# Attention's probabilities times values: from split float32r on the whole array to plain float32 on two column halves

## The chip, the core and the metric

The kernel runs on one core of a Trainium2 chip. A core has five engines with a queue of instructions each: TensorE (PE in the profile, with its weight loads as PEld), VectorE (DVE), ScalarE (ACT), GpSimd (POOL) and SyncE (SP), which here issues the DMAs. Arrays lie in SBUF, 128 partitions with a free axis; TensorE writes to PSUM only, here six tiles that the kernel calls banks. The metric is device time in microseconds (us) of one execution, the median of several runs. One execution was also taken with the hardware profiler; all durations below are from it.

## What is computed

Two layers of a hybrid mixer, over 1024 latent tokens and 256 context tokens of width 1024. One input projection feeds a convolution branch, windowed attention and a gated linear attention (GLA); each branch has its own gate, and an output projection ends the layer. What matters here is the attention:

```python
def one_block(args):                       # 128 queries, 8 heads, 2 kv heads
    qn, kn, vn, mn = args
    s_loc = jnp.einsum('bqhgd,bkhd->bhgqk', qn, kn).astype(F32)
    s_loc = jnp.where(mn, s_loc, NEG_INF)
    s_ctx = jnp.einsum('bqhgd,bchd->bhgqc', qn, kc).astype(F32)
    p = jax.nn.softmax(jnp.concatenate([s_sink, s_ctx, s_loc], axis=-1), axis=-1)
    return (jnp.einsum('bhgqc,bchd->bqhgd', p_ctx, vc)
            + jnp.einsum('bhgqk,bkhd->bqhgd', p_loc, vn))
b_l = _windowed_attention(...) * jax.nn.silu(pl['b_gate'])
```

A block of 128 queries looks at the 256 context tokens and at its own, the previous and the next 128 tokens. In layer 0 the two context blocks attend as well, to the context alone. Everything is float32.

## The kernel before

The kernel is written as some dozens of generators ("lanes") which a planner runs (`Hybrid.loop`, lines 201 to 228). `Model` (lines 49 to 154) holds an estimated clock of each engine and, for every eight columns of a buffer, when it will be written and read; a lane yields what it waits for, and the planner resumes the lane with the smallest priority number among those that are ready at the model's PE clock, or else the one that will be ready first. The order in which instructions are issued is therefore set at build time by these estimates. A matmul with a `tile_position` is priced at its full cost times its share of the columns plus 29 ns (line 141); the model has no price for going from whole-array matmuls to tiled ones and back.

Precise products use float32r, a float32 type that TensorE takes in one pass. An operand is split into a high part (rounded to float32r) and a low part (what is left), and three products, high-high, high-low and low-high, are summed (`three`, line 673); `split` (line 362) does it with a copy and a subtraction.

The attention phase of a layer starts at `attn_start` (line 1187). Its units are (query block, kv head) with four heads each: 20 in layer 0, 16 in layer 1. A unit (`u_run`, line 1304) makes scores for four heads (`u_score`), takes exponentials and sums (`u_head`), scales them, and then goes over its 128-token key tiles, 5 for an inner block, 4 for a border block, 2 for a context block, which is 84 pairs of unit and key tile in layer 0 and 76 in layer 1, 160 in all. For each pair four TensorE transposes (one per head) fill a PSUM bank with 128 keys by 512 (head, query) columns. `u_ev` (line 1379) brings the bank to SBUF as a PT buffer of 1024 columns: ACT copies it, halved, into float32r, then DVE subtracts that copy from the bank to get the low part. `u_pv` (line 1388) multiplies: the stationary operand is `vst`, 128 keys by 128 columns that hold the high and the low part of one kv head's values, and the moving operand is the high and then the low half of PT, two matmuls of 512 columns that accumulate over the unit's key tiles in a bank `O`. Rows 0 to 63 of `O` then hold the high values' products and rows 64 to 127 the low values'; ACT copies the lower half out, DVE adds the halves (twice, one for each parity of the head), and DVE or POOL multiplies the result into the gate in `mix`.

The values get to `vst` by `v_prep` (line 1253): a DMA from the DRAM tensor `kd` to a small buffer, then a split. There are 3 PT buffers, cut from `H1`, the 8192-column float32r tile that held the projection's input for tokens 0 to 511; they are free once its last reader, the gate group `(7, 1)` in `phase_a`, has been issued (flag `h1out`). `H1` also holds the odd query tile, and `hi` and `ml`, the split operands of the output projection (`out_tiles`, line 1469).

Lanes of priority below the units' (2 and up) are `u_pv` (1.8), `u_ev` (1.7), `u_head` (1.9) and the preparation of keys and queries (1); the gate groups (9) and the output projection (8) fill in. Banks for transposes are limited to 3 at a time during the gate groups and after (`CAPB`, `CAPC`), accumulators to 2 and then 3.

Of the kernel before, what the change touches and what calls it, by code (L numbers as in the profile page):

```python
# [9 lines left out]
F32 = mybir.dt.float32  # L10
F32R = mybir.dt.float32r
# [153 lines left out]
class Hybrid:  # L165
# [361 lines left out]
    def views(self):  # L527

        self.HC = self.tile("HC", 4096, F32R)
        self.H2 = [self.tile(f"H2_{k}", 4096, F32R) for k in range(2)]  # L530
        for k in range(3):
            self.slots["PT"].append((0.0, self.H1[:, 2560 + 1024 * k:3584 + 1024 * k]))
        self.hc = self.HC.rearrange("p (s k t) -> p s k t", s=2, k=8)
        self.h2 = [x.rearrange("p (s k t) -> p s k t", s=2, k=4) for x in self.H2]

    def H(self, c, hl, k, a, n):
        if c == 0:
            return self.hc[:, hl, k, a:a + n]
        if c == 1:
            return self.h1[:, hl, k, a:a + n]  # L540
        return self.h2[k // 4][:, hl, k % 4, a:a + n]

    def rstd(self, ss, scale, n):
# [14 lines left out]
    def part_h(self, l, i, k0, n, x):  # L558

        nc = self.nc  # L560
        c, a = self.hslot(i)
        st = 1 if i < 2 else 0
        mods = tuple(f"mod{l}.{m + k // 2}" for m in (0, 4) for k in range(k0, k0 + n, 2))
        yield mods if n == 2 else mods[0]
        yield self.bank_need("tr")
        tp = self.bank_get("tr")
        for b in range(n):
            nc.tensor.transpose(tp[:, b * 128:(b + 1) * 128], x[:, b * 128:(b + 1) * 128], self.idf)
        yield None, self.need("SM"), mods, f"hfree{l}{c}"
        h = self.sm(128 * n)  # L570
        v = []
        for b in range(n):
            k = k0 + b
            v.append((h[:, b * 128:(b + 1) * 128], tp[:, b * 128:(b + 1) * 128],
                      self.modc[:, l, 8 + k, st:st + 1], self.modc[:, l, k, st:st + 1]))

        def on_dve():
            for o, p, s, f in v:
                nc.vector.tensor_scalar(o, p, s, f, op0=ALU.mult, op1=ALU.add)

        def on_act():
            for o, p, s, f in v:
                nc.scalar.activation(o, p, ACTF.Identity, scale=s, bias=f)
        self.pick(("dve", 320 * n, on_dve), ("act", 345 * n, on_act))
        self.free(tp)
        yield
        t = self.h2[k0 // 4][:, :, k0 % 4:k0 % 4 + n] if c == 2 else (self.hc if c == 0 else self.h1)[:, :, k0:k0 + n]
        self.split(t[:, 0, :, a:a + 128], t[:, 1, :, a:a + 128], h.rearrange("p (b t) -> p b t", b=n))
        self.free(h)
        for k in range(k0, k0 + n, 2):  # L590
            self.flag(f"h{l}.{i}.{k // 2}")
# [595 lines left out]
    def attn_start(self, l):  # L1187

        nc = self.nc
        kv = self.H1  # L1190
        self.kst = self.HC[:, 0:3072].rearrange("p (v s t) -> p v s t", v=2, s=2)
        self.vst = kv[:, 0:1536].rearrange("p (t v c) -> p t v c", t=6, v=2)
        self.Q = [x.rearrange("p (h t) -> p h t", h=8) for x in (self.HC[:, 3072:4096], kv[:, 1536:2560])]
        self.ml = kv[:, 7680:8192].rearrange("p (a b t) -> p a b t", a=2, b=2)
        yield self.need("SM", 1, 0, True), tuple(f"{x}{l}.{i}" for x in ("kv", "q0", "q1") for i in range(2, NT))
        self.rope_free()
        self.amask = self.sm(640)
        self.rsv = True
        nc.sync.dma_start(self.amask, self.I["amask"])
        self.go(self.gate_rows(l), 3)  # L1200
        ctx = [0, 1] if l == 0 else []
        blocks = list(range(2, NT)) + ctx if CTXL else ctx + list(range(2, NT))
        prev = None
        for n, i in enumerate(blocks):
            for kv in range(2):
                u = self.unit(l, n, i, kv, prev)
                self.units.append(u)
                u.lane = self.go(self.u_run(u), 2 + 0.01 * len(self.units))
                prev = u
        self.outs = self.go(self.out_proj(l, blocks), 8)  # L1210
        done = set()
        for n, i in enumerate(blocks):
            for t in self.keys(i):
                if t not in done:
                    done.add(t)
                    yield f"kv{l}.{t}", lambda: 0.0 if self.pre < 4 else None
                    self.pre += 1
                    self.go(self.kv_prep(l, t, blocks.index(t - 3) if t >= 6 else None), 1)
            yield f"q0{l}.{i}", f"q1{l}.{i}", lambda: 0.0 if self.pre < 4 else None
            self.pre += 1  # L1220
            self.go(self.q_prep(l, n, i), 1)
# [29 lines left out]
        self.flag(f"k{l}.{i}")  # L1251

    def v_prep(self, l, i, used):
        nc = self.nc
        j = self.kslot(i)
        yield self.need("SM", 1, PK), f"h1out{l}", *used
        x = self.sm_spare(128)
        nc.sync.dma_start(x, self.kd[i, :, 128:256])
        yield self.at(x)
        self.split(self.vst[:, j, :, 0:64], self.vst[:, j, :, 64:128], x.rearrange("p (v d) -> p v d", v=2))  # L1260
        self.free(x)
        self.flag(f"kv{l}.{i}.v")

    def q_prep(self, l, n, i):
# [114 lines left out]
    def u_ev(self, u, q, tp, PT):  # L1379
        nc = self.nc  # L1380
        yield self.at(tp)
        nc.scalar.activation(PT[:, 0:512], tp, ACTF.Copy, scale=0.5)
        yield
        nc.vector.scalar_tensor_tensor(PT[:, 512:1024], tp, 0.5, PT[:, 0:512].bitcast(F32), op0=ALU.mult, op1=ALU.subtract)
        self.free(tp)
        u.PT[q] = (PT, nc.end)

    def u_pv(self, u):
        nc = self.nc
        nk = len(u.keys)  # L1390
        O = None
        for q in range(nk):
            yield lambda: u.PT[q][1] if q in u.PT else None, (0.0 if q else self.bank_need("ac"))
            if q == 0:
                O = self.bank_get("ac")
            PT = u.PT[q][0]
            for s in range(2):
                nc.tensor.matmul(O, self.vst[:, self.kslot(u.keys[q]), u.kv], PT[:, s * 512:(s + 1) * 512], start=(q == 0 and s == 0),
                                 stop=(q == nk - 1 and s == 1))
            self.free(PT)  # L1400
        yield None, self.need("SM"), tuple(f"bg{u.l}.{2 + 2 * u.kv}.{j}.{self.hslot(u.i)[0]}" for j in (0, 1))
        tt = self.sm(512)
        nc.scalar.activation(tt[0:64], O[64:128], ACTF.Copy)
        yield
        O4 = O.rearrange("p (a b t) -> p a b t", a=2, b=2)
        t4 = tt.rearrange("p (a b t) -> p a b t", a=2, b=2)
        for b in (1, 0):
            nc.vector.tensor_tensor(t4[64 * b:64 * b + 64, :, 0], O4[0:64, :, b], t4[0:64, :, b], op=ALU.add)
        self.free(O)
        yield  # L1410
        c = col(u.i * 128)
        g = self.mix(slice(2 + 2 * u.kv, 4 + 2 * u.kv), slice(c, c + 128))
        self.pick(("dve", 345, lambda: nc.vector.tensor_tensor(g, g, t4[:, :, 0], op=ALU.mult)),
                  ("pool", 690, lambda: nc.gpsimd.tensor_tensor(g, g, t4[:, :, 0], op=ALU.mult)))
        self.free(tt)
        self.flag(f"u{u.key}")


# [50 lines left out]
    def out_tiles(self, l, blocks, par, lanes):  # L1469
        yield  # L1470
        for n, i in list(enumerate(blocks))[par::2]:
            early = par == 0 and n < len(blocks) - 4
            lanes[par].prio = 8 + 0.01 * n
            if l == 0 and n >= len(blocks) - 2:
                a = 256 + 256 * par
                hi = self.HC[:, 0:3072].rearrange("p (a c) -> p a c", a=4)[:, :, a:a + 256].rearrange("p a (b t) -> p a b t", b=2)
                free = f"sc{l}.{len(blocks) - 3}"
            else:
                a = 5632 + 1024 * par
                hi = self.H1[:, a:a + 1024].rearrange("p (a b t) -> p a b t", a=4, b=2)  # L1480
                free = f"h1out{l}"
            yield (self.need("SM", 2 - early, 1), f"u{l}.{n}.0", f"u{l}.{n}.1", free, f"gb{l}",
                   f"ln{l}{self.hslot(i)[0]}", self.rest(hi), (self.rest(self.ml) if early else 0.0))
# [88 lines left out]
    def phase_a(self, l):  # L1572
# [9 lines left out]
        for g in GROUPS[:-1]:  # L1582
# [34 lines left out]
            else:  # L1617
# [4 lines left out]
                for n, (p, c) in enumerate(B_GATE):  # L1622
# [2 lines left out]
                    yield from self.t_group(l, p, self.ev_gate(l, 2 * p - 10), cx, order=(c,), last=all(x[0] != p for x in B_GATE[n + 1:]))  # L1625
                    if n == MODG:
                        self.flag("mods")
                    if p == 7:
                        self.flag({0: f"hcfree{l}", 1: f"h1out{l}", 2: f"h2out{l}"}[c])

    def phase_bc(self, l):
# [8 lines left out]
                self.go(self.x_next(i), 1 + 0.01 * ((i - 2) % NT))  # L1640
        yield tuple(u.lane for u in self.units), f"ml{l}.0", f"ml{l}.1"
        self.slots["SF"] = []
        self.flag(f"hfree{l + 1}1")
        self.free(self.amask)
        yield self.outs
# [9 lines left out]
    def run(self):  # L1655
        nc, I = self.nc, self.I
        self.w, self.gk, self.zs = {}, {}, {}
        with self.tc.manual_schedule():
            self.consts()
            self.stat = self.sb.tile([128, 4, 2, 4], F32, name="stat")  # L1660
            self.mix_new(F32)
            self.H1 = self.tile("H1", 8192, F32R)
            self.h1 = self.H1.rearrange("p (s k t) -> p s k t", s=2, k=8)
            self.flag("hfree01")

            def x_load(i):
# [73 lines left out]
PK = 1  # L1740
# [95 lines left out]
```

## Time and profile before

| | |
|---|---|
| median of 3 runs | 1324.24 us (1323.89 to 1325.28) |
| the profiled execution | 1324.96 us, span of its core 1323.2 us |
| PE busy | 1245.2 us, 94% of the span |
| PEld / DVE / ACT / POOL busy | 1085.2 / 931.4 / 600.4 / 490.8 us |
| granted TensorE clock, mean | 0.985 of full speed |
| attention of layer 0, of layer 1 | about 440 to 700 us and 1080 to 1290 us of the span |

A matmul's row begins when its columns start into the array and has an end that is modelled, so rows of successive matmuls overlap: a matmul of 256 columns is listed with some 280 ns although the next one starts 120 ns later. What a matmul costs PE is therefore read from start to start. In the profile one float32 matmul counts as two instructions (two passes), a float32r matmul and a transpose as one. Line 43 is the helper through which every instruction is issued, so rows are told apart by their tiles: `H` stands for H1 and H2 (numbers are left out), `SM` are small work buffers, `idr` is the identity of a transpose, `WS` weights, `mix` the gates and branch outputs.

### The profile page before, as it was taken

What the parts mean: (1) busy time and instruction counts of PE and PEld (TensorE: products, weight loads), DVE (VectorE), ACT (ScalarE), POOL (GpSimd) and SP (SyncE); (2) the same over time, 40 slices, a digit from 0 to 9 for tenths busy, and PEclk for the clock granted to TensorE, in tenths of its full rate; (3) what the DMA queues carried; (4) which work ended last, traced back from release to release, by engine and by line L of the source; (5) the groups of instructions that cost most, each with busy time, mean ns of one, the idle gap of its engine ahead of it and who ended that gap; (6) DMA issues with size and microseconds to landing.
All of it is one profiled execution on the core that took longest, in us unless ns stands there. A gap on an engine that the chain in (4) does not pass through costs nothing. (4 is left out here: it accounts for less than half of the span.)

```text
span 1323.2 us, 24344 instructions
## 1 busy us (share of the span) xinstructions
PE 1245.2 (94%) x9198; PEld 1085.2 (82%) x9198; DVE 931.4 (70%) x1756; ACT 600.4 (45%) x1355; POOL 490.8 (37%) x657
## 2 busy tenths in 40 slices
PE   5999998999999999899999899989999999899997
PEld 3668987888887777779988779878888888799887
DVE  5836896886364578767686677897864667987874
ACT  3721441254323456457664451431343256776641
POOL 1410054754133335434441231064651344455420
PEclk9999998999999999999999999989999999999999
DMA  9443113222014243431114521114321131211012
GB/s 327 153 140 118 48 41 96 57 76 79 28 44 142 92 131 99 138 109 51 49 57 144 182 90 59 45 42 116 85 64 56 44 97 41 87 62 53 33 65 80
DMA packets 113238, 116.48 MB, mean 88 GB/s; under 512 B 38464, under 2 KB 81760, under 8 KB 113120
## 3 DMA queue, kind: packets, MB, share of 16 engines
q1 hardware_dynamic: 113120, 114.92, 28.3%
q8 instruction: 72, 1.18, 0.4%
q14 instruction: 46, 0.38, 0.1%
HBM read 95.47 MB, written 19.42 MB: 87 GB/s over the span
## 5 line engine op out<-in xcount | busy, mean ns | idle before, releaser
L43 PE MATMUL ps<-H,WS 128*128 128x512 f32 x1344 | 338.0, 399 | 3.3 <-ACT U L43 1.7
L43 PEld LDWEIGHTS ps<-H,WS 128*128 128x128 f32 x1344 | 245.2, 189 | 62.2 <-issue 8.8
L43 PE MATMUL ps<-WS,H 128*128 128x256 f32 x1704 | 256.6, 292 | 6.6 <-DVE H L43 3.5
L43 PEld LDWEIGHTS ps<-WS,H 128*128 128x128 f32 x1704 | 229.4, 195 | 20.0 <-issue 10.3
L43 ACT ACTIVATE SM<-ps 128x512 f32<-128x512 f32 (+3 forms) x180 | 93.0, 517 | 333.8 <-PE ps L43 291.9
L43 DVE SCALAR_TENSOR_TENSOR mix<-U,small,mix 128x1295 f32<-128x1295 f32 (+1 forms) x120 | 177.8, 1522 | 0.0
L43 PE MATMUL ps<-idr,SM 128*128 128x128 f32 (+1 forms) x1076 | 150.1, 272 | 26.8 <-POOL SM L43 14.2
L43 PEld LDWEIGHTS ps<-idr,SM 128*128 128x128 f32 (+1 forms) x1076 | 124.3, 143 | 51.3 <-POOL SM L43 17.2
L43 ACT ACTIVATE SM<-SM,stat 128x641 f32<-128x641 f32 (+2 forms) x144 | 110.6, 769 | 50.5 <-DVE stat L43 38.0
L43 DVE SCALAR_TENSOR_TENSOR H<-ps,H 128x512 fp32r<-128x512 f32 x160 | 106.0, 682 | 38.1 <-ACT H L43 37.8
L43 ACT ACTIVATE H<-ps 128x512 fp32r<-128x512 f32 x174 | 98.6, 597 | 73.6 <-PE ps L43 63.7
L43 DVE CUSTOM_DVE_ANT_0 SM<-ps,SM,small 128x640 f32<-128x640 f32 (+2 forms) x128 | 102.5, 810 | 29.1 <-PE ps L43 28.4
L43 POOL TENSOR_TENSOR tir<-tir,mhalf 128x1 f32<-128x1 f32 (+2 forms) x55 | 46.5, 851 | 178.8 <-DVE tir L43 154.1
L43 POOL TENSOR_TENSOR SM<-SM,SM 128x128 fp32r<-128x128 f32 (+3 forms) x58 | 58.6, 1018 | 130.8 <-ACT SM L43 108.9
L43 PE MATMUL ps<-H 128*128 128x512 f32 x320 | 97.5, 406 | 1.4 <-DVE H L43 1.3
L43 PE MATMUL ps<-H,H 128*128 128x256 f32 x552 | 98.2, 286 | 0.2 <-DVE H L43 0.2
L43 ACT ACTIVATE SM<-SM 32x128 f32<-32x128 f32 (+4 forms) x200 | 72.0, 368 | 41.2 <-DVE SM L43 33.5
L43 PE MATMUL ps<-SM,SM 128*32 128x128 f32 (+4 forms) x764 | 79.2, 288 | 7.5 <-ACT SM L43 3.9
L43 PEld LDWEIGHTS ps<-H,H 128*128 128x128 f32 x552 | 82.0, 189 | 2.1 <-DVE H L43 0.5
L43 POOL TENSOR_SCALAR SM<-SM,tir 128x640 f32<-128x640 f32 (+2 forms) x77 | 64.7, 853 | 34.5 <-DVE tir L43 23.9
L43 POOL TENSOR_TENSOR SM<-SM,WR 128x256 f32<-128x256 f32 (+2 forms) x66 | 69.0, 1051 | 16.0 <-DVE SM L43 5.8
L43 POOL TENSOR_TENSOR WR<-SM,SM 128x256 f32<-128x256 f32 (+1 forms) x48 | 45.5, 969 | 72.1 <-ACT SM L43 72.1
(151 smaller groups left out, 2133.3 us busy)
## 6 DMA issues: line engine op xcount, KB each, us to landing
WR<-in_w_in_dram SPq DMA_DIRECT2D x80, 256.0 KB, 3.7
WR<-in_w_mod_dram SPq DMA_DIRECT2D x64, 256.0 KB, 3.1
WR<-in_w_out_dram SPq DMA_DIRECT2D x32, 256.0 KB, 3.3
SM<-vd SPq DMA_DIRECT2D x116, 64.0 KB, 2.5
x<-SM SPq DMA_DIRECT2D x20, 256.0 KB, 2.4
SM<-x SPq DMA_DIRECT2D x20, 256.0 KB, 4.0
qd<-SM SPq DMA_DIRECT2D x18, 256.0 KB, 2.4
mix<-in_x_dram SPq DMA_DIRECT2D x8, 512.0 KB, 8.3
```

What stands on the lines that cost most here:

```text
L43: r = getattr(self._e, op)(*a, **k)
```

## The change

`H1` becomes two tiles of 4096 columns, one for the high and one for the low part. When gate group `(7, 1)` has been issued, the high one is taken again as a float32 tile (`h1_keep`): 768 columns for the values and six PT buffers of 512 columns. The odd query tile, `hi` and `ml` move to the low one. Probabilities and values are no longer split. `v_prep` becomes one DMA from `kd` straight to `vst`. `u_ev` becomes one copy, halved, on ACT or on DVE, whichever the planner expects to end first. In `u_pv` each key tile has two float32 matmuls of 256 columns: heads of even parity go to array columns 0 to 63, those of odd parity to columns 64 to 127 (`tile_position`), so that `O` gets 128 rows and 256 columns, and one DVE multiplication from PSUM into the gate ends the unit. The transposes, scores, softmax and projections are not edited; since the planner's estimates change, the order in which everything is issued may change too.

```diff
-        for k in range(3):
-            self.slots["PT"].append((0.0, self.H1[:, 2560 + 1024 * k:3584 + 1024 * k]))
...
+    def h1_keep(self):
+        self.h1_new(0, F32)
+        x = self.H1[0]
+        self.vst = x[:, 0:768].rearrange("p (t v c) -> p t v c", t=6, v=2)
+        for k in range(6):
+            p = x[:, 768 + 512 * k:1280 + 512 * k]
+            self.slots["PT"].append((self.nc.touched(p), p))
...
     def v_prep(self, l, i, used):
-        nc = self.nc
-        j = self.kslot(i)
-        yield self.need("SM", 1, PK), f"h1out{l}", *used
-        x = self.sm_spare(128)
-        nc.sync.dma_start(x, self.kd[i, :, 128:256])
-        yield self.at(x)
-        self.split(self.vst[:, j, :, 0:64], self.vst[:, j, :, 64:128], x.rearrange("p (v d) -> p v d", v=2))
-        self.free(x)
+        yield f"h1out{l}", *used
+        self.nc.sync.dma_start(self.vst[:, self.kslot(i)], self.kd[i, :, 128:256].rearrange("p (v c) -> p v c", v=2))
...
     def u_ev(self, u, q, tp, PT):
-        nc.scalar.activation(PT[:, 0:512], tp, ACTF.Copy, scale=0.5)
-        yield
-        nc.vector.scalar_tensor_tensor(PT[:, 512:1024], tp, 0.5, PT[:, 0:512].bitcast(F32), op0=ALU.mult, op1=ALU.subtract)
+        self.pick(("act", 135 + 512 / 1.4, lambda: nc.scalar.activation(PT, tp, ACTF.Copy, scale=0.5)),
+                  ("dve", 75 + 512 / 0.96, lambda: nc.vector.tensor_scalar(PT, tp, 0.5, None, op0=ALU.mult)))
...
     def u_pv(self, u):
...
-            for s in range(2):
-                nc.tensor.matmul(O, self.vst[:, self.kslot(u.keys[q]), u.kv], PT[:, s * 512:(s + 1) * 512], start=(q == 0 and s == 0),
-                                 stop=(q == nk - 1 and s == 1))
+            p4 = PT.rearrange("p (a b t) -> p a b t", a=2, b=2)
+            for b in range(2):
+                nc.tensor.matmul(O[64 * b:64 * b + 64], self.vst[:, self.kslot(u.keys[q]), u.kv], p4[:, :, b], start=(q == 0),
+                                 stop=(q == nk - 1), tile_position=(0, 64 * b))
             self.free(PT)
-        yield None, self.need("SM"), tuple(f"bg{u.l}.{2 + 2 * u.kv}.{j}.{self.hslot(u.i)[0]}" for j in (0, 1))
-        tt = self.sm(512)
-        nc.scalar.activation(tt[0:64], O[64:128], ACTF.Copy)
...
-        for b in (1, 0):
-            nc.vector.tensor_tensor(t4[64 * b:64 * b + 64, :, 0], O4[0:64, :, b], t4[0:64, :, b], op=ALU.add)
...
-        self.pick(("dve", 345, lambda: nc.vector.tensor_tensor(g, g, t4[:, :, 0], op=ALU.mult)),
-                  ("pool", 690, lambda: nc.gpsimd.tensor_tensor(g, g, t4[:, :, 0], op=ALU.mult)))
+        nc.vector.tensor_tensor(g, O, g, op=ALU.mult)
...
-                a = 5632 + 1024 * par
-                hi = self.H1[:, a:a + 1024].rearrange("p (a b t) -> p a b t", a=4, b=2)
+                a = 1024 + 1024 * par
+                hi = self.H1[1][:, a:a + 1024].rearrange("p (a b t) -> p a b t", a=4, b=2)
...
+                    if (p, c) == (7, 1):
+                        self.h1_keep()
...
+        if l == 0:
+            self.slots["PT"] = []
+            self.h1_new(0, F32R)
```

## Rows read from the trace of the kernel before

**Rows 1.** The page: busy time; then 40 equal slices, in tenths.
```profile
PE 1245.2 (94%) x9198; PEld 1085.2 (82%) x9198; DVE 931.4 (70%) x1756; ACT 600.4 (45%) x1355; POOL 490.8 (37%) x657
...
PE   5999998999999999899999899989999999899997
...
PEclk9999998999999999999999999989999999999999
```

**Rows 2.** Busy time by stretch: the two attentions, the ends of the layers.
```profile
core 0: us, PE busy (x) PEld busy (x) DVE busy (x) ACT busy (x) POOL busy (x), PEclk, DMA share, GB/s
440.00:700.00 260.00, 249.60 (x1789) 215.74 (x1788) 191.11 (x409) 154.61 (x340) 109.51 (x184) 0.99 0.30 95
1080.00:1290.00 210.00, 200.37 (x1431) 181.77 (x1430) 168.49 (x345) 139.26 (x296) 95.86 (x156) 1.00 0.18 59
```

**Rows 3.** Groups of instructions: busy us, mean ns of one, idle before.
```profile
L43 PE MATMUL ps<-H 128*128 128x512 f32 x320 | 97.5, 406 | 1.4 <-DVE H L43 1.3
...
L43 DVE SCALAR_TENSOR_TENSOR H<-ps,H 128x512 fp32r<-128x512 f32 x160 | 106.0, 682 | 38.1 <-ACT H L43 37.8
...
L43 DVE TENSOR_TENSOR SM<-ps,SM 64x256 f32<-64x256 f32 x72 | 30.1, 418 | 11.3 <-ACT SM L43 9.2 <-issue 1.0
...
L43 DVE CAST HC<-ps 128x512 fp32r<-128x512 f32 x6 | 4.1, 687 | 6.0 <-PE ps L43 6.0
...
L43 ACT ACTIVATE H<-ps 128x512 fp32r<-128x512 f32 x174 | 98.6, 597 | 73.6 <-PE ps L43 63.7 <-DVE stat L43 4.4 <-DVE H L43 3.5
```

**Rows 4.** Timeline of PE: one product amid output projection, layer 1.
```profile
1258.18 0.40 PE L43 MATMUL ps<-WS,H 128*128 128x256 f32 x2
1258.41 0.28 PE L43 MATMUL ps<-WS,SM 128*128 128x256 f32 x1
1258.53 0.40 PE L43 MATMUL ps<-WS,H 128*128 128x256 f32 x2
1258.77 0.28 PE L43 MATMUL ps<-WS,SM 128*128 128x256 f32 x1
1258.88 0.63 PE L43 MATMUL ps<-H 128*128 128x512 f32 x2
1259.35 0.63 PE L43 MATMUL ps<-HC,H 128*128 128x256 f32 x4
```

**Rows 5.** Timeline of PE in GLA: column-half products amid a projection.
```profile
253.46 1.08 PE L43 MATMUL ps<-SM,SM 128*64 128x256 f32 x8
254.48 1.69 PE L43 MATMUL ps<-WS,HC 128*128 128x256 f32 x12
256.10 1.08 PE L43 MATMUL ps<-SM,SM 128*64 128x256 f32 x8
257.01 0.40 PE L43 MATMUL ps<-mix,SM 128*64 128x64 f32 x4
...
277.24 0.65 PE L43 MATMUL ps<-SM,SM 128*64 128x256 f32 x4 [0.64 <-ACT SM L43]
277.82 1.45 PE L43 MATMUL ps<-WS,H 128*128 128x256 f32 x10
...
315.76 1.52 PE L43 MATMUL ps<-SM,SM 128*64 128x256 f32 x12
```

**Rows 6.** Timeline of PE: first and last runs of attention's products.
```profile
447.97 0.63 PE L43 MATMUL ps<-H 128*128 128x512 f32 x2
...
448.73 1.16 PE L43 MATMUL ps<-H 128*128 128x512 f32 x4
449.72 1.35 PE L43 MATMUL ps<-idr,SM 128*128 128x128 f32 x12
...
1283.57 0.63 PE L43 MATMUL ps<-H 128*128 128x512 f32 x2
```

**Rows 7.** Waits of PE's weight loads, 440 to 700, then 1080 to 1290.
```profile
PEld ps L43 <- ACT ps L43: 5.9, 4, 2.4
PEld ps L43 <- DVE H L43: 3.1, 5, 1.2
PEld ps L43 <- ACT H L43: 2.0, 6, 0.4
...
PEld ps L43 <- DVE H L43: 9.8, 13, 2.1
PEld ps L43 <- DVE stat L43: 3.6, 7, 0.8
```

More of the change, by code (lines that the diff above doesn't have):

```diff
@@ L530, in views, with h1_new @@
         self.H2 = [self.tile(f"H2_{k}", 4096, F32R) for k in range(2)]
-        for k in range(3):
-            self.slots["PT"].append((0.0, self.H1[:, 2560 + 1024 * k:3584 + 1024 * k]))
         self.hc = self.HC.rearrange("p (s k t) -> p s k t", s=2, k=8)
         self.h2 = [x.rearrange("p (s k t) -> p s k t", s=2, k=4) for x in self.H2]
+    def h1_new(self, s, dt):
+        t, old = self.tile(f"H1_{s}", 4096, dt), self.H1[s]
+        if old is not None:
+            m, b = self.nc.part(t)
+            m[1, b] = self.nc.touched(old)
+        self.H1[s] = t
+        if dt == F32R:
+            self.h1[s] = t.rearrange("p (k t) -> p k t", k=8)
+    def h1_keep(self):
[5 more added lines that the diff above has]
+            self.slots["PT"].append((self.nc.touched(p), p))
     def H(self, c, hl, k, a, n):
@@ L539, in H @@
         if c == 1:
-            return self.h1[:, hl, k, a:a + n]
+            return self.h1[hl][:, k, a:a + n]
         return self.h2[k // 4][:, hl, k % 4, a:a + n]
@@ L586, in part_h @@
         yield
-        t = self.h2[k0 // 4][:, :, k0 % 4:k0 % 4 + n] if c == 2 else (self.hc if c == 0 else self.h1)[:, :, k0:k0 + n]
-        self.split(t[:, 0, :, a:a + 128], t[:, 1, :, a:a + 128], h.rearrange("p (b t) -> p b t", b=n))
+        if c == 1:
+            t = [x[:, k0:k0 + n, a:a + 128] for x in self.h1]
+        else:
+            t = [(self.h2[k0 // 4][:, s, k0 % 4:k0 % 4 + n] if c else self.hc[:, s, k0:k0 + n])[:, :, a:a + 128] for s in range(2)]
+        self.split(*t, h.rearrange("p (b t) -> p b t", b=n))
         self.free(h)
@@ L1189, in attn_start @@
         nc = self.nc
-        kv = self.H1
         self.kst = self.HC[:, 0:3072].rearrange("p (v s t) -> p v s t", v=2, s=2)
-        self.vst = kv[:, 0:1536].rearrange("p (t v c) -> p t v c", t=6, v=2)
-        self.Q = [x.rearrange("p (h t) -> p h t", h=8) for x in (self.HC[:, 3072:4096], kv[:, 1536:2560])]
-        self.ml = kv[:, 7680:8192].rearrange("p (a b t) -> p a b t", a=2, b=2)
+        self.Q = [x.rearrange("p (h t) -> p h t", h=8) for x in (self.HC[:, 3072:4096], self.H1[1][:, 0:1024])]
+        self.ml = self.H1[1][:, 3072:3584].rearrange("p (a b t) -> p a b t", a=2, b=2)
         yield self.need("SM", 1, 0, True), tuple(f"{x}{l}.{i}" for x in ("kv", "q0", "q1") for i in range(2, NT))
@@ L1390, in u_pv @@
         nk = len(u.keys)
-        O = None
+        bank = None
         for q in range(nk):
@@ L1394, in u_pv @@
             if q == 0:
-                O = self.bank_get("ac")
+                bank = self.bank_get("ac")
+                O = bank[:, 0:256].rearrange("p (a t) -> p a t", a=2)
             PT = u.PT[q][0]
-            for s in range(2):
-                nc.tensor.matmul(O, self.vst[:, self.kslot(u.keys[q]), u.kv], PT[:, s * 512:(s + 1) * 512], start=(q == 0 and s == 0),
-                                 stop=(q == nk - 1 and s == 1))
+            p4 = PT.rearrange("p (a b t) -> p a b t", a=2, b=2)
+            for b in range(2):
+                nc.tensor.matmul(O[64 * b:64 * b + 64], self.vst[:, self.kslot(u.keys[q]), u.kv], p4[:, :, b], start=(q == 0),
+                                 stop=(q == nk - 1), tile_position=(0, 64 * b))
             self.free(PT)
-        yield None, self.need("SM"), tuple(f"bg{u.l}.{2 + 2 * u.kv}.{j}.{self.hslot(u.i)[0]}" for j in (0, 1))
-        tt = self.sm(512)
-        nc.scalar.activation(tt[0:64], O[64:128], ACTF.Copy)
-        yield
-        O4 = O.rearrange("p (a b t) -> p a b t", a=2, b=2)
-        t4 = tt.rearrange("p (a b t) -> p a b t", a=2, b=2)
-        for b in (1, 0):
-            nc.vector.tensor_tensor(t4[64 * b:64 * b + 64, :, 0], O4[0:64, :, b], t4[0:64, :, b], op=ALU.add)
-        self.free(O)
-        yield
+        yield None, tuple(f"bg{u.l}.{2 + 2 * u.kv}.{j}.{self.hslot(u.i)[0]}" for j in (0, 1))
         c = col(u.i * 128)
         g = self.mix(slice(2 + 2 * u.kv, 4 + 2 * u.kv), slice(c, c + 128))
-        self.pick(("dve", 345, lambda: nc.vector.tensor_tensor(g, g, t4[:, :, 0], op=ALU.mult)),
-                  ("pool", 690, lambda: nc.gpsimd.tensor_tensor(g, g, t4[:, :, 0], op=ALU.mult)))
-        self.free(tt)
+        nc.vector.tensor_tensor(g, O, g, op=ALU.mult)
+        self.free(bank)
         self.flag(f"u{u.key}")
@@ L1661, in run @@
             self.mix_new(F32)
-            self.H1 = self.tile("H1", 8192, F32R)
-            self.h1 = self.H1.rearrange("p (s k t) -> p s k t", s=2, k=8)
+            self.H1, self.h1 = [None, None], [None, None]
+            for s in range(2):
+                self.h1_new(s, F32R)
             self.flag("hfree01")
```

## The prediction

> **What bounds the kernel now.** I began with the page's busy times [rows 1]: PE is busy for 94% of the span and its granted clock is full nearly everywhere, while DVE, the next, stands at 70%. Then the stretches [rows 2]. The change touches only the two attention phases. In the first PE is busy for 249.6 of 260 us, in the second for 200.4 of 210, with DVE at 191.1 and 168.5. So DVE is loaded but PE is the engine that runs out of time, and an edit is worth what it does to PE: its own work, or its waits. Next the waits of PE's queue in the two stretches [rows 7]: what PE waits for among the attention's own products (a PT half that DVE or ACT has still to write, named H) is 3.1 + 2.0 + 9.8 = 14.9 us; the rest of the list is bank copies and softmax statistics, 5.9 and 3.6 us in the largest rows. The reader is to see that the large DVE group (160 subtractions, 106.0 us, [rows 3]) is hidden behind PE except for those 14.9 us.
>
> **What a product costs PE before.** From start to start [rows 4]: projection matmuls of 256 columns follow each other at 0.117 us (1258.18 to 1258.53, three of them). The product of one key tile, two float32r matmuls of 512 columns, takes 1258.88 to 1259.35, 0.47 us, and nothing is lost before or after it. The 160 of them are about 75 us; the 97.5 us of [rows 3] contain waits and overlaps.
>
> **What it costs after.** GLA already has the same thing: float32, 256 columns, 64 array columns, the two halves in turn [rows 5]. Four records are one pair of such matmuls, which is what one key tile will need. A group of 4 lasts 0.65 us, of 8 1.08, of 12 1.52: each further pair adds (1.52 - 0.65)/2 = 0.435 us, that is, two steps of some 0.217 us for four passes. The two halves do run side by side. Streaming gains 0.47 - 0.435 = 0.035 us for a key tile, 160 x 0.035 = 5.6 us. It is small because a float32 matmul takes two passes at half the column rate of the float32r one, so packing only pays back what the wider type costs.
>
> **What lies between.** In [rows 5] a group of 8 and 12 projection matmuls run from 253.46 to 256.10, 2.64 us. The 12 take 12 x 0.118 = 1.42 us at the pace of [rows 4], the two pairs 0.87; 0.35 us are left. This is lost once for every excursion from whole-array matmuls to halves and back: the first half-array product starts late, and so does the first whole-array one after it (277.24 to 277.82 is 0.58 us for a lone pair of 0.435). Where a half-array group is followed by another half-array one nothing is lost: 256.10 to 257.01 is 0.91 us for two pairs, against 1.02 from 253.46 to 254.48. I take 0.34. [...]
>
> **How many excursions.** Attention's products stand in the PE timeline in 117 runs, the first and the last of them in [rows 6]: 81 of one key tile, 29 of two, 7 of three. Between them are transposes, scores, gates and output projection, all on the whole array. With this order the loss is 117 x 0.34 = 39.8 us. The order won't stay. A PT buffer is ready after one copy (597 ns on ACT, 687 on DVE, by the nearest rows) in place of a copy and a subtraction (597 + 682) [rows 3], and there are six instead of three, so transposes run further ahead and more products can be ready together; against this, a product that is ready has a better priority than the next transposes and goes at once, and the transposes have at most three banks. If four go together and the last alone, each of the 32 units with 4 or 5 keys has two runs and the four context units one: 68. If every key tile goes alone it is 160. I take three for an inner unit (24 units), 2.4 for a border one (8) and one for a context one (4): 72 + 19 + 4 = 95, hence 95 x 0.34 = 32.3 us.
>
> **What is removed elsewhere.** DVE loses 160 subtractions (106.0 us) and 72 additions (30.1 us) [rows 3], and gets 36 multiplications from PSUM (some 0.42 us each, as the additions of 256 columns are: 15 us) and perhaps half the copies (80 x 0.687 = 55 us): about 66 us less. ACT loses 36 copies of `O` and up to half the PT copies. All of that lies beside PE's work and is worth what PE waited for it. Lower end 0 (PE, slower itself, waits for its turn anyway), upper end the whole of both lists' engine waits, which I put at twice the 14.9 us; I take 14.9, since exactly the waits named H lose a step of 0.68 us and a hop between engines. What is late next is PE. The chain at a unit's end (copy, two additions, multiplication) becomes one multiplication; it holds a bank and releases the output projection, which has other tiles to go on with, so I put it at nothing, with a bound of 1.7 us (0.60 + 2 x 0.42 + 0.69 - 0.42) at each layer's last unit, if that cover is gone.
>
> **The rest at nothing.** `v_prep` loses a split off the path. Its DMA now waits for the last products that read the slot, in SP's queue, and behind it stand loads of weights, queries and residuals; it is issued after the unit that used the slot was issued to its end, so PE is at most a few matmuls away: 0, bound 2 us a layer. The H1 halves are freed and taken at the same flags as before: 0. Re-planned order outside the attention: 0, with 3 us to each side by the look of PE's waits.
>
> **The sum.** -5.6 + 32.3 - 14.9 = +11.8 us on the profiled 1324.96 us, 1336.8; that execution lies 0.7 above the median, so 1336 against 1324.24. About 0.2%, 2.6 us, is what a measurement of this kernel can tell from no change.
>
> **Rivals.**
> *The products run in long runs and the waits go* (faster). Two runs in a unit, 68 x 0.34 = 23.1; -5.6; and 25 us of waits gone, since six buffers take PE clear of DVE: -7.5, 1317. For it: three PT buffers do throttle the transposes now, and 14.9 us of waits have just this name. Against it: the ready product overtakes the transposes. It decides below some 60 to 75 runs, where the loss equals streaming and waits together. Chance 0.2. Around its edge lies no change (75 runs with 20 us of waits regained: -0.1, 1324): 0.1.
> *The products go one by one* (slower still). 160 x 0.34 = 54.4 - 5.6 - 10 = +39, 1363; 130 runs give +29, 1353. For it: short readiness, high priority. Against: a projection step of six or twelve matmuls, 1.4 us by [rows 4], lets two become ready. Chance 0.15.
> *The halves don't run side by side.* Then a pair takes 0.87 us and 160 x 0.435 = 70 us more come on top: 1406. [Rows 5] speak against it with the same shape and order. Chance 0.02.
> The forecast has what is left, 0.53, between +3 and +25 us.
>
> **Numbers.** Faster 0.2, same 0.1, slower 0.7. The range, 8 in 10: the lower end is the rival of long runs, 1317; the upper reaches past 117 runs with 14.9 us back (39.8 - 5.6 - 14.9 = +19, 1343) and with nothing back (+34, 1358), so 1317 to 1358.
>
> **What would show it.** In the profile after: 640 records of 256 columns on 128*64, in pairs that start together and four of them in some 0.435 us; the starts just before and just after each run late by 0.1 us and the following slot too; PE's waits for H near zero; DVE some 66 us less busy and the span not shorter by that. The count of runs is the weakest step. The prediction is wrong if there are many fewer than 68 of them, if the loss is hidden (an excursion that falls where PE would have waited), or if the waits that vanish are several times 14.9 us.

## The result, and the profile after

The changed kernel takes 1334.92 us (median of 4 runs, 1333.02 to 1335.66) against 1324.07 for the kernel before on the same chip (4 runs): 1.0078 of it, 95% interval 1.0061 to 1.0095, 10.9 us slower. A second measurement, on another chip (e12 below), gave 1.0043 (1.0017 to 1.0069), some 6 us slower. The forecast was 1336. The profiled execution has a span of 1331.2 us.

The page of the changed kernel, busy times and slices, answers [rows 1]:

```profile
PE 1256.9 (94%) x9518; PEld 1064.3 (80%) x9518; DVE 831.9 (62%) x1566; ACT 563.6 (42%) x1279; POOL 463.7 (35%) x615
...
PE   5999988999999999999999799979999999999997
...
PEclk9999998999999999999999899999999999999999
```

DVE lost 99.5 us, ACT 36.8, POOL 27.1, and PE gained 11.7. The engines that were relieved are not the one that sets the time.

The groups of the changed kernel (busy us, mean ns, idle before) that take the place of those in [rows 3]:

```profile
L43 PE MATMUL ps<-H 128*64 128x256 f32 x640 | 86.7, 392 | 0.2 <-ACT H L43 0.2
...
L43 ACT ACTIVATE H<-ps 128x512 f32<-128x512 f32 x135 | 75.4, 598 | 61.9 <-PE ps L43 61.4
...
L43 DVE TENSOR_SCALAR H<-ps 128x512 f32<-128x512 f32 x25 | 16.9, 687 | 24.1 <-PE ps L43 23.6 <-ACT SM L43 0.4
...
L43 DVE TENSOR_TENSOR mix<-ps,mix 128x256 f32<-128x256 f32 x36 | 15.2, 421 | 39.2 <-PE ps L43 38.4 <-ACT H L43 0.8
```

The 86.7 us of busy time look better than the 97.5 of [rows 3]. That is the trap: the time lost in changing the array's form (from the whole array to column halves and back) is in no group. It shows from start to start. The PE timeline of the changed kernel, a lone product amid the output projection, to be laid beside [rows 4], and then a run of five key tiles:

```profile
1166.78 0.92 PE L43 MATMUL ps<-WS,H 128*128 128x256 f32 x6
1167.63 0.65 PE L43 MATMUL ps<-H 128*64 128x256 f32 x4
1168.21 0.50 PE L43 MATMUL ps<-WS,H 128*128 128x256 f32 x2
1168.55 0.28 PE L43 MATMUL ps<-WS,SM 128*128 128x256 f32 x1
...
576.42 2.38 PE L43 MATMUL ps<-H 128*64 128x256 f32 x20
578.73 0.66 PE L43 MATMUL ps<-idr,SM 128*128 128x128 f32 x4
```

The lone product holds PE for 0.58 us (0.47 before), it starts 0.14 us after the six projection matmuls (6 x 0.118) should have ended, and the two matmuls behind it take 0.34 in place of 0.24. Five together take 2.31: each further key tile adds 0.432.

One thing that the change of form takes away is the head start of the weights. The weight loads around the same lone product:

```profile
1167.63 0.20 PEld L43 LDWEIGHTS ps<-H 128*64 128x64 f32 x4
1168.21 0.30 PEld L43 LDWEIGHTS ps<-WS,H 128*128 128x128 f32 x2 [0.39 <-issue]
1168.44 0.19 PEld L43 LDWEIGHTS ps<-WS,SM 128*128 128x128 f32 x1
```

The load of the matmul at 1168.55 starts 0.11 us ahead of it. The first load for the halves and the first for the whole array after them start only with their own matmuls, at 1167.63 and 1168.21. So it is at all 80 runs of products on the way in, and at all but one on the way out: the lead is 0.001 to 0.003 us, where the kernel before has a median of 0.112 and 0.229 at its 117 runs.

Waits of PE's weight loads in the changed kernel, 440 to 700 and then 1080 to 1300, beside [rows 7]:

```profile
PEld ps L43 <- issue: 29.5, 84, 2.5
PEld ps L43 <- ACT H L43: 2.3, 8, 0.4
...
PEld ps L43 <- DVE H L43: 0.5, 2, 0.4
...
PEld ps L43 <- issue: 15.1, 45, 0.4
PEld ps L43 <- DVE stat L43: 8.4, 10, 2.6
PEld ps L43 <- ACT H L43: 2.4, 8, 0.5
```

The waits for DVE's part of PT are gone (DVE H, 12.9 to 0.5 us); those for ACT's copies (ACT H) have grown from 2.0 to 4.7, and those of layer 1's scores for DVE's softmax reductions from 3.6 to 8.4. The largest row, "issue" (idle time in which the weight loads wait for nothing that the profile shows), has grown from 10.0 to 29.5 us in the first stretch and from 0.4 to 15.1 in the second.

### The profile page after: what moved, and what is told of

It is laid out like the page before. It is cut to its first block, busy times and chain, and to the rows that moved or that the text cites. A ratio compares the mean times of both kernels' runs of the same rounds, so it can differ in the third digit from the quotient of the medians.

```text
span 1331.2 us, 24579 instructions
## 1 busy us (share of the span) xinstructions
PE 1256.9 (94%) x9518; PEld 1064.3 (80%) x9518; DVE 831.9 (62%) x1566; ACT 563.6 (42%) x1279; POOL 463.7 (35%) x615
## 5 line engine op out<-in xcount | busy, mean ns | idle before, releaser
L43 PE MATMUL ps<-WS,H 128*128 128x256 f32 x1704 | 253.0, 290 | 0.0
L43 ACT ACTIVATE SM<-ps 128x512 f32<-128x512 f32 (+3 forms) x144 | 71.4, 496 | 311.6 <-PE ps L43 270.3
L43 PEld LDWEIGHTS ps<-idr,SM 128*128 128x128 f32 (+1 forms) x1076 | 121.0, 142 | 63.1 <-POOL SM L43 20.5
L43 ACT ACTIVATE H<-ps 128x512 f32<-128x512 f32 (+1 forms) x152 | 84.8, 598 | 74.1 <-PE ps L43 73.6
L43 POOL TENSOR_SCALAR SM<-SM,tir 128x640 f32<-128x640 f32 (+2 forms) x89 | 73.7, 842 | 53.3 <-DVE tir L43 42.2
L43 PE MATMUL ps<-H 128*64 128x256 f32 x640 | 86.7, 392 | 0.2 <-ACT H L43 0.2
L43 POOL TENSOR_TENSOR SM<-SM,WR 128x256 f32<-128x256 f32 (+2 forms) x61 | 63.9, 1053 | 31.6 <-DVE SM L43 23.9
L43 PE MATMUL ps<-WS,SM 128*128 128x256 f32 x248 | 70.1, 283 | 1.1 <-DVE SM L43 1.1
```

The lines of the kernel that those rows point to most:

```text
L43: r = getattr(self._e, op)(*a, **k)
```

## The experiments

All ratios below are to the kernel before on the same chip; 0.001 is 1.3 us. "Runs" are the stretches in which attention's products follow each other on PE, counted in the order of issue: 117 before, 80 in the changed kernel. The theory under test: the time goes into excursions from the whole array to its column halves, 80 of some 0.3 us, less a small gain in streaming and a gain in waits. The rival: the float32 product or the new order costs the time. Four of the experiments leave out part of the result: e7 and e8 the odd heads, e4 the low part of the probabilities, and e5 adds odd and even heads together.

**Excursions taken out, order kept (e7).**

```diff
-            for b in range(2):
-                nc.tensor.matmul(O[64 * b:64 * b + 64], self.vst[:, self.kslot(u.keys[q]), u.kv], p4[:, :, b], start=(q == 0),
-                                 stop=(q == nk - 1), tile_position=(0, 64 * b))
+            v = self.vst[:, self.kslot(u.keys[q])]
+            nc.nc.tensor.matmul(O, v.rearrange("p v c -> p (v c)"), p4[:, :, 0], start=(q == 0), stop=(q == nk - 1))
+            for b in range(2):
+                nc.issue("pe", "matmul", (O[64 * b:64 * b + 64], v[:, u.kv], p4[:, :, b]), dict(tile_position=(0, 64 * b)))
```

> The changed kernel in exactly its own order of issue, but each key tile has one float32 product of 256 columns on the whole array (both kv heads' values against the even heads) in place of the two on the column halves: the same two passes of 0.216 us, no excursion. The odd heads are left out. If the excursions cost their row price, 80 x 0.30 = 24 us go and it takes some 0.990 of the kernel before, 1311 us on a chip where that takes 1324; if a quarter of them fall where PE would have waited, as the tiny products suggest, 18 us go: 1317. If the halves are not what costs time, it stays at the changed kernel's 1335.

Measured: 0.988 (0.9846 to 0.9914), 1313.2 us. Against the changed kernel's 1.0043 and 1.0078 that is 0.016 to 0.020, 22 to 26 us for 80 excursions, 0.27 to 0.33 us each (with the intervals, and as the two ran on different chips, 16 to 31 us). Its timeline has three key tiles in 1.29 us, 0.43 each, with nothing lost around them, and its weight loads wait for "issue" as little as in the kernel before (440 to 700, then 1080 to 1300):

```profile
1109.33 1.46 PE L1413 MATMUL ps<-H 128*128 128x256 f32 x6
1110.62 1.04 PE L43 MATMUL ps<-idr,SM 128*128 128x128 f32 x8
```

```profile
PEld ps L43 <- issue: 11.1, 34, 0.4
...
PEld ps L43 <- issue: 0.4, 1, 0.4
```

So the whole loss of the change is the excursions: without them, everything else that it does would be worth 0.012, 16 us (11 to 20). Of this, streaming is 160 x (0.47 - 0.432) = 6 us, and some 10 us (5 to 14) are left for waits and order, which this run doesn't separate.

**An excursion by itself (e2, with e3 as control).** In the kernel before, ahead of each head's scores (the first line is e2's, the second e3's):

```diff
+        nc.nc.tensor.matmul(S[0:64, 0:2], self.idf[:, 0:64], self.idf[:, 0:2], start=True, stop=True, tile_position=(0, 0))
+        nc.nc.tensor.matmul(S[:, 0:2], self.idf, self.idf[:, 0:2], start=True, stop=True)
```

> The kernel before, with one tiny extra float32 product (2 columns, 64 array columns at column half 0) ahead of each head's scores: 144 of them, unknown to the planner, so that the order of everything else is that of the kernel before. Its result is not used. If going to the halves and back costs 0.30 to 0.35 us each time, this is 43 to 50 us slower than the same kernel with a tiny whole-array product (e3). If switching costs nothing and only the work counts, it is no slower than that one.

> The control: the kernel before with the same tiny product on the whole array (128 array columns, 2 moving columns, float32), 144 times. Only two weight loads that have little to hide behind: about 0.1 to 0.15 us each time, 14 to 22 us over the kernel before, under either theory.

Measured: e2 1.0327 (1.0298 to 1.0357), e3 1.0202 (1.0174 to 1.023). The difference is 0.0125, 17 us, not 43 to 50, and e3 alone takes 27 us, not 14 to 22: the expectations took the price of an excursion to come on top of that of the tiny product. The timelines, e2 first:

```profile
601.67 0.28 PE L43 MATMUL ps<-WS,SM 128*128 128x256 f32 x1
601.88 0.28 PE L1350 MATMUL ps<-idr 128*64 128x2 f32 x2
602.09 0.85 PE L43 MATMUL ps<-HC,H 128*128 128x256 f32 x4
```

```profile
600.91 0.28 PE L43 MATMUL ps<-WS,SM 128*128 128x256 f32 x1
601.03 0.28 PE L1350 MATMUL ps<-idr 128*128 128x2 f32 x2
601.17 0.83 PE L43 MATMUL ps<-HC,H 128*128 128x256 f32 x4
```

A product of two columns on the half array starts 0.21 us after its predecessor's start (0.12 on the whole array) and the next work starts 0.21 after it (0.14); but on the whole array too it delays what follows. What e2 settles is the sum: 144 excursions with next to nothing in them cost 0.0327, 43 us, 0.30 us each. How much of that is weights that nothing hides and how much another part of the change of form, the pair doesn't separate; e7 shows that both go when the array stays whole.

**Both products in one half (e5).**

```diff
-                O = bank[:, 0:256].rearrange("p (a t) -> p a t", a=2)
+                O = bank[0:64, 0:256].rearrange("p (a t) -> p a t", a=2)
...
-                nc.tensor.matmul(O[64 * b:64 * b + 64], ..., start=(q == 0), stop=(q == nk - 1), tile_position=(0, 64 * b))
+                nc.tensor.matmul(O, ..., start=(q == 0 and b == 0), stop=(q == nk - 1 and b == 1), tile_position=(0, 0))
```

> The changed kernel in its own order, but both products of a key tile go to column half 0, one after the other (even and odd heads are summed there, and only rows 0 to 63 of the gate are multiplied). If the halves run side by side in the changed kernel, as its rows show, each key tile takes 0.43 us more here: 160 x 0.43 = 69 us, about 1.06 of the kernel before, 1404 us. If they don't, nothing changes: 1335.

Measured: 1.0482 (1.0446 to 1.0518), 0.040 to 0.044 above the changed kernel: 54 to 58 us. PE's busy time in these products goes from 86.7 to 155.3 us:

```profile
L43 PE MATMUL ps<-H 128*64 128x256 f32 x640 | 155.3, 385 | 0.2 <-ACT H L43 0.2
```

The halves do run side by side: that saves PE 69 us of busy time and the span 54 to 58, where 69 had been expected. Why some 12 us of it don't reach the span was not shown; waits that PE has anyway may cover them.

**Fewer excursions (e1), and the same without them (e8: this edit and e7's).**

```diff
-            yield lambda: u.PT[q][1] if q in u.PT else None, (0.0 if q else self.bank_need("ac"))
+            if q == 0:
+                yield lambda: max(x[1] for x in u.PT.values()) if len(u.PT) == nk else None, self.bank_need("ac")
```

> The changed kernel, but a unit's products wait until all its PT buffers are written, so that they are issued in one run: 35 runs in the order of issue instead of 80. If the loss is a fixed price for each excursion to the column halves (0.30 us), 45 of them less are 13.5 us less: about 1321.5 us, faster than the kernel before. If the changed kernel's extra time comes from something else (the float32 product itself, the new order, other waits), fewer runs bring nothing, and the later product and the later release of the PT buffers cost a few us: 1335 to 1342.

> The kernel with one run for a unit (e1), again in exactly its order of issue, with the same whole-array product in place of the halves. 35 excursions go, 35 x 0.33 = 11.5 us. If the one-run order itself is what ate its gain, it stays above the one with the changed kernel's order (e7) by the 13 us that fewer excursions should have brought: about 1.000 to 1.003 of the kernel before. If the order is as good as the other, both come out alike, at 0.990 to 0.995.

Measured: e1 1.0096 (1.0065 to 1.0127), e8 1.0012 (0.9989 to 1.0034). e1 missed the 1321.5 us that fewer excursions alone would give. The 35 excursions left are worth 0.0084, 11 us, 0.32 each, which again is the price (across two chips, with the intervals, 6 to 16 us); but e8 lies 0.013, 17 us, above e7, which differs from it by the order alone. The 45 excursions saved were paid back by that order. The profiles say in which stage: from layer 0's first score to the first `ps<-H,HC` matmul, near the layer's end, e8's profiled execution takes 310.7 us and e7's 295.3. Within it, busy time from 525 to 555 us, the changed kernel first, then e1:

```profile
525.00:555.00 30.00, 26.87 (x223) 22.42 (x222) 14.18 (x30) 17.83 (x40) 15.66 (x24) 1.00 0.30 93
```

```profile
525.00:555.00 30.00, 22.92 (x133) 18.35 (x132) 14.19 (x27) 9.08 (x21) 14.24 (x16) 0.77 0.19 60
```

In e1 PE gets 133 matmul instructions done here in place of 223, and the granted clock is 0.77 of full speed. The PE timeline of e1 and the waits in this stretch say why:

```profile
534.02 1.12 PE L43 MATMUL ps<-H,H 128*128 128x256 f32 x8
...
536.74 0.39 PE L43 MATMUL ps<-H,H 128*128 128x256 f32 x1 [1.14 <-DVE H L43]
538.14 1.10 PE L43 MATMUL ps<-H,H 128*128 128x256 f32 x7 [1.01 <-POOL H L43]
...
541.62 0.58 PE L43 MATMUL ps<-H,H 128*128 128x256 f32 x1 [1.56 <-DVE H L43]
543.02 0.58 PE L43 MATMUL ps<-H,H 128*128 128x256 f32 x1 [0.82 <-POOL H L43]
...
543.61 0.63 PE L43 MATMUL ps<-H,H 128*128 128x256 f32 x2
544.03 0.41 PE L43 MATMUL ps<-H,SM 128*128 128x256 f32 x1
544.25 0.63 PE L43 MATMUL ps<-H,H 128*128 128x256 f32 x2
```

```profile
ACT WS L43 <- DMA WR<-in_w_out_dram: 14.6, 1, 14.6
...
DVE H L43 <- DMA WR<-in_w_out_dram: 7.3, 3, 4.4
...
PEld ps L43 <- DVE H L43: 4.2, 3, 1.9
...
PEld ps L43 <- POOL H L43: 3.4, 3, 1.2
```

The matmuls `ps<-H,H` and `ps<-H,SM` are layer 0's output projection, whose weights are still arriving, piece by piece (DMA, then the split on DVE or POOL). In e1 PE's timeline has nothing else here, and each piece is waited for in the open. After the first two of these gaps the granted clock falls to 0.50 of full speed for 13.7 us, and the three matmuls from 543.61 to 544.25 take 0.64 us instead of 0.35 (3 x 0.117, [rows 4]):

```profile
539.20:552.90 13.70, 9.76 (x41) 7.42 (x41) 3.18 (x6) 2.04 (x5) 6.12 (x5) 0.50 0.19 58
```

In the changed kernel the same projection begins earlier, at 525.77 us, and its weights are still arriving too, but between its pieces lie transposes and `ps<-HC` products, as its PE timeline shows:

```profile
532.89 0.48 PE L43 MATMUL ps<-H,H 128*128 128x256 f32 x2
533.21 0.28 PE L43 MATMUL ps<-H,SM 128*128 128x256 f32 x1
...
533.69 0.46 PE L43 MATMUL ps<-idr,SM 128*128 128x128 f32 x4
533.98 1.62 PE L43 MATMUL ps<-HC 128*128 128x256 f32 x12
535.45 0.60 PE L43 MATMUL ps<-idr,SM 128*128 128x128 f32 x4
535.80 0.48 PE L43 MATMUL ps<-H,H 128*128 128x256 f32 x2
```

So it is the mixture, as I read it, that the products' later readiness spoils. That this stretch holds all of the 17 us was not shown; the clock's part in it is, by an estimate from its 0.50 over 13.7 us, at most half of them, some 7 us. From 525 to 555 us the changed kernel's granted clock is 1.00. In e1 two gaps of 1.14 and 1.01 us, with a matmul between them, come before the fall: the second ends at 538.14, the stretch at 0.50 begins at 539.20. That the gaps bring the clock down was not shown: the changed kernel has a gap of 2.08 us ahead of 552.08, and its clock stays at 1.00.

**Three PT buffers (e6).**

```diff
-        for k in range(6):
+        for k in range(3):
```

> The changed kernel with three PT buffers instead of six: 85 runs of products in the order of issue, against 80. If six buffers were what shortened the waits and let products run together, it is 5 to 12 us slower than the changed kernel. If the single copy did that, the five runs more cost 1.5 us and nothing else changes: 1334 to 1338.

Measured: 1.0198 (1.0169 to 1.0227), 0.012 to 0.016 above the changed kernel: 16 to 21 us, more than either theory gave. Five more excursions are 1.5 of them. Its stretch from 530 to 560 us shows the same dry stretch as in e1, with the granted clock at 0.72:

```profile
530.00:560.00 30.00, 23.05 (x129) 17.74 (x127) 5.37 (x10) 6.90 (x15) 9.09 (x11) 0.72 0.27 83
```

From layer 0's first score to the first `ps<-H,HC` matmul it takes 323.4 us, the changed kernel 308.2. So the number of buffers matters through the order that it lets the planner make, not through the count of runs.

**Without the subtraction (e4).** In the kernel before:

```diff
-        yield
-        nc.vector.scalar_tensor_tensor(PT[:, 512:1024], tp, 0.5, PT[:, 0:512].bitcast(F32), op0=ALU.mult, op1=ALU.subtract)
...
-                nc.tensor.matmul(O, self.vst[:, self.kslot(u.keys[q]), u.kv], PT[:, s * 512:(s + 1) * 512], ...
+                nc.tensor.matmul(O, self.vst[:, self.kslot(u.keys[q]), u.kv], PT[:, 0:512], ...
```

> The kernel before without the subtraction in u_ev: the low part of the probabilities is left out and the high part is multiplied twice, so PE's work is as before (320 matmuls of 512 columns) and DVE has 106 us less. If the waits for the PT halves are worth what they show, 14.9 us, it takes about 1309 us. If DVE was hidden and the waits only move to the next thing that is late (scores, banks), 1317 to 1324.

Measured: 0.9949 (0.9931 to 0.9968), 7 us less (4 to 9). With 106 us of subtractions gone (DVE's busy time falls by 92, as the planner moves other work to it) the kernel gains 7, half of the 14.9 that the waits show. It is not the subtraction by itself: the planner has new estimates here too, and attention's products stand in 99 runs in place of 117. In the second attention, from 1080 to 1300, the waits for DVE's part of PT (9.8 us) are gone from the list, and others stand at its head:

```profile
PEld ps L43 <- POOL SM L43: 5.8, 8, 1.4
PEld ps L43 <- DVE stat L43: 4.2, 7, 1.5
```

These were 1.1 and 3.6 in the kernel before. As in the changed kernel, PE waits for the next thing that is late, softmax.

**Two runs for a unit (e9), with a planner that knows the price (e10), in layer 1 alone (e11).** The changed kernel itself ran beside them (e12). The lines are e9's, then some of what e10 adds, where `mode` is 128 for a whole-array matmul and the size of the tile otherwise.

```diff
+            if q == 0 or q in (2,):
+                ks = [k for k in range(nk) if k >= q and (k == q or not any(q < s <= k for s in (2,)))]
+                yield lambda: max(u.PT[k][1] for k in ks) if all(k in u.PT for k in ks) else None, (0.0 if q else self.bank_need("ac"))
...
+                if mode != self.mode:
+                    x += 170
+                self.mode = mode
```

> The changed kernel with a unit's products in at most two runs: key tiles 0 and 1 together, then the rest together; 56 runs in the order of issue instead of 80. By the price of an excursion, 24 x 0.33 = 8 us less than the changed kernel, if the order does no harm: 1.002 of the kernel before. If waiting for a group lets PE run dry, as with one run for a unit, the gain is eaten: 1.008 or more.

> As e9, and the planner is told a price for every change between whole-array and tiled matmuls (0.17 us each way) and 0.43 us for a pair on the column halves; 55 runs. If the planner's wrong clock is what lets PE run dry, this is faster than e9: 0.998 to 1.002 of the kernel before. If not, it is as e9 within 5 us.

> Two runs a unit in layer 1 alone; layer 0 plans as in the changed kernel; 68 runs. 12 x 0.33 = 4 us less than the changed kernel if layer 1's order does no harm: 1.005 of the kernel before. Else 1.008 to 1.010.

> The changed kernel itself on the chip of these runs, for comparison: 1.0078 of the kernel before, as in the first measurement, between 1.005 and 1.011.

Measured: e9 0.9982 (0.9965 to 0.9999), e10 1.0143 (1.0112 to 1.0173), e11 1.0041 (1.0013 to 1.0069), e12 1.0043. e12 lies just below the 1.005 to 1.011 that it was given. e9 has 24 excursions less than e12 and is 0.006, 8 us (4 to 12), faster: 0.33 each, as expected, though its order is another as well; it is level with the kernel before, or a shade faster. e11 gained nothing that can be told from noise. e10 missed: 55 excursions, yet 21 us slower than e9. Busy time from 556 to 606 us, e9 first, then e10:

```profile
556.00:606.00 50.00, 48.01 (x371) 35.24 (x369) 29.06 (x62) 33.74 (x74) 22.00 (x38) 1.00 0.34 105
```

```profile
556.00:606.00 50.00, 41.78 (x279) 33.88 (x279) 26.42 (x53) 23.87 (x50) 22.21 (x29) 0.83 0.36 108
```

Once more layer 0's attention has gaps, and the clock is at 0.83. From layer 0's first score to the first `ps<-H,HC` matmul e10 takes 320.2 us, e9 300.9. The price of 0.17 us each way did not bring a better order; it holds for GLA's tiled matmuls too, so that e10 differs from e9 outside the attention as well, and what the planner lacks there was not pursued.

## Why the prediction was right, step by step

*What bounds the kernel.* Right: 99.5 us less of DVE and 36.8 of ACT came with a slower kernel, and e4 gives 7 us for 92 us of DVE.

*The price of a product and the streaming gain.* Right: 0.432 us for a further key tile, 0.435 forecast; the side-by-side halves are shown by e5.

*The price of an excursion.* 0.34 forecast from GLA's rows. By the rows it is 0.35 where a projection follows and about 0.30 where transposes do, since they lose 0.05 less at the exit (from the first to the second transpose 0.165 us in place of 0.109, between a projection's first two matmuls 0.222 in place of 0.118); by the runs 0.27 to 0.33 (e7 against e12 and the changed kernel), 0.32 (e1 against e8), 0.33 (e9), each with an interval of about a third of it to either side, or more; the rows are the closer measure. The forecast was slightly too high, for the neighbours were not weighed: 45 of the 80 runs are followed by transposes.

*How many excursions.* 95 forecast, 80 counted (35 of one key tile, 25 of two, 20 of three to six). The reasoning did not hold, that shorter readiness and a high priority pull the products apart and six buffers join them. Three buffers (e6) give 85 runs, so that six join five; and a single copy in the kernel before, with its three buffers (e4), gives 99 in place of 117, so that with shorter readiness more products go together there, not fewer. What the rest of the drop comes from was not isolated. Term: 32.3 forecast, 80 x 0.31 = 25 us by the rows, 22 to 26 by e7.

*Waits regained.* 14.9 forecast, about 10 measured (e7: 16 less 6 of streaming, which holds the new order too). This term and that of the excursions were both too large, by 5 and 7 us: the two errors nearly cancel, and the forecast came out at 1336 with a sum that is really -6 + 25 - 10 = +9. That it met the first measurement to about 1 us is luck; the second gave 6 us. Two things failed in the term. The waits named H were not all waits of attention's own products: by the rows only 3.4 of the 14.9 us stand ahead of a product's weights, while 4.8 stand ahead of transposes and 3.8 ahead of projection matmuls, ended by the subtraction that reads a bank. And "what is late next is PE": of the 14.9 us 5.2 are still there, now mostly for ACT's copies, and in layer 1 the scores wait longer for DVE's reductions (3.6 to 8.4 us); e4 shows the same of the scores.

*DVE.* 66 us less forecast, 99.5 measured: the planner put 135 of the 160 copies on ACT, not half. Without weight, as DVE was covered.

*Re-planned order, put at 0 with 3 us to each side.* Too narrow as a bound: e1, e6 and e10 show that a change of this size in what is ready can cost 15 to 20 us, nearly all in layer 0's attention and output projection, where PE has gaps and the granted clock is lower in the same stretches (0.77, 0.72 and 0.83). In the changed kernel itself the order's part was not separated; with the waits it comes to a gain of some 10 us (e7).

*The rivals.* The one by one order did not come, the halves do run side by side. The rival of long runs named the right lever: e9, with 56 runs, ends at 0.998, near its edge (no change at 60 to 75 runs with the waits regained).

## What to carry to other kernels

Before packing small products into column halves, count how often the array must change its form, and read the price from start to start around an existing tiled product; the group's busy time hides it. Here some 0.3 us for each excursion outweighed a gain of 0.04 us for each key tile and 10 us of waits and order, until nearly three key tiles shared one excursion (e9: 160 / 56 = 2.9). And take an engine's relief at the waits it removes, less what is late next, not at its busy time.

## What was not expected of the hardware

Two columns of float32 on the whole array, without any change of form, cost 27 us for 144 products, 0.19 us each (e3). Its rows show why: the tiny product's two weight loads start at 600.92 us and the next product's at 601.14, so that the loads take 0.22 us with next to no streaming above them. At a change of form, too, the weight load no longer runs ahead of its matmul (0.002 us in place of 0.112 and 0.229); whether that is the whole price was not separated. And the granted clock is part of the price of an order: a stretch of e1 with gaps of 0.7 to 1.6 us between matmuls, with PE still listed as busy for 23 of 30 us, ran at 0.77, and matmuls of 256 columns there at 0.21 us in place of 0.12.
